# A transformer layer in split fp32r: negations later, low parts by accumulating DMA, a projection kept in HBM

## The chip, the cores and the metric

One core of a Trainium2 chip runs the whole program. The metric is the device time of one execution in microseconds. The kernel before takes 702.74 us (median of three runs, 701.41 to 702.83). TensorE (PE) multiplies, VectorE (DVE) and ScalarE (ACT) work element by element, GpSimd (POOL) has a few small operations and one DMA queue, and SyncE (SP) has the other DMA queue.

## The reference, cut to what matters

One layer on 512 tokens of width 1024, in float32, with 21 inputs:

```python
h = rms_norm(x, g_mix); z = h @ w_in      # w_in: 1024 x 3136, split into eight parts
a = mla(...)        # 4 heads: low-rank q and kv, QK-norm, rotary, dense softmax
r = hgrn2(...)      # 4 heads: gated linear recurrence in both directions, chunks of 64
x = x + concat(a, r) @ w_o
h = rms_norm(x, g_ffn)
x = x + (silu(h @ w_gate) * (h @ w_up)) @ w_down      # width 2816 inside
gate = sigmoid(rms_norm(x, g_ple) @ w_ple_gate)
x = x + gate * (p @ w_ple_proj)           # p: 512 x 256, the embeddings of the layer
```

## The kernel before, in words

Everything is held transposed: features on the 128 partitions, the 512 tokens along the free dimension. Each float32 matrix is split into a high part, rounded to the fast type fp32r, and a low part, the rest. `mm3` (L141) makes one product of three matmuls: high by high, high by low, low by high (L142, L143, L144).

A weight's parts come about in one of two ways. `split` (L132) copies the loaded tile to the high part on ScalarE (L135) and subtracts on VectorE (L136). The other way needs no VectorE: a negated copy of the high part goes into the low part's tile (ScalarE), and a DMA on GpSimd's queue loads the weight once more and adds it to that tile.

The mixer (attention, recurrence, and the products with w_in and w_o) takes its weights in 30 chunks of 1024 columns by `weights` (L148) from rings of four tiles each (WB), two chunks by `split`, 28 by DMA. `wnext` (L602) keeps three chunks ahead (AHEAD) and hands out the oldest: the call for chunk n asks for chunk n + 2. In before this includes the high part's DMA (L155), the negation (L156) and the accumulating DMA (L157), one after the other. `w_in_tile` (L608) uses a chunk in 24 matmuls, `w_in_tokens` (L621) two chunks at a time for the recurrence's values, `w_o_half` (L880) the output projection. Chunks 1 to 6 and 7 to 12 are gates and queries for two heads each, 13 to 16 values, 17 to 20 output gates, 21 to 24 and 27 to 30 w_o, 25 and 26 the projection of the embeddings. This dense stream and the latency-bound stream of attention (L373) and recurrence are generators that `merge` (L93) interleaves by their progress.

After the mixer, the feed-forward runs over 22 tiles of 128 inner features in six parts of 4, 4, 4, 4, 3 and 3. The four of part 0 (`pair_plain`, L1036) load w_gate and w_up in halves of 512 columns (`halves`, L1019) and multiply plainly; `block_sums` (L1074) forms on the side the sums of the activations that the other 18 tiles (`pair_seven`, L1096) need, where seven products of half the width take the place of eight. `down_weights` (L1154) and `down` (L1176) add each part's down projection to x. The last stage multiplies by w_ple_gate (from L1232), takes the sigmoid and the product with the embeddings' projection, and stores.

All [128, 512] tiles outside the mixer's weight rings are slots from one first-in, first-out ring (`Slots`, L58): `A` with 74 slots, to which 22 more are joined when the mixer's rings are given up. A tile that is asked for takes the slot that was given back longest ago, and its writer waits for that slot's last reader. In before the eight tiles of the embeddings' projection (`pp`, written at L952, read at L1247) keep eight slots through the whole feed-forward.

The order of the instructions on each engine and queue is not that of the program text: a planner runs a simulated timeline with its own costs when the kernel is built, takes at each moment what is ready by it, earlier text first, and fixes each queue's order; on the chip each queue then runs in that order and waits on semaphores. `issue_after` and the matmuls in `marks` pin single instructions behind others.

## Time and profile before

| what | before |
|---|---|
| median of three runs | 702.74 us |
| the profiled execution | 700.41 us |
| its span, from the first to the last instruction | 698.6 us |
| PE busy | 686.4 us, 98% |
| PE weight loads busy | 604.2 us, 86% |
| DVE busy | 509.5 us, 73% |
| ACT busy | 383.2 us, 55% |
| POOL busy | 111.1 us, 16% |
| moved by DMA | 91.18 MB, 131 GB/s on average |

Busy time of matmuls counts their modelled ends, so a pause between two matmuls is longer from start to start than in the idle column. The mixer lasts to some 295 us of the span, the plain pairs to some 350, the rest of the feed-forward to some 648, the last stage to the end.

### The profile page before, as it was taken

How to read it: one execution, taken by the hardware profiler on the slowest of the kernel's cores; microseconds unless marked ns; L12 is line 12 of the kernel's file. 1: busy time of each engine (PE TensorE's matmuls, PEld its weight loads, DVE VectorE, ACT ScalarE, POOL GpSimd, SP SyncE). 2: the span in 40 equal slices, each digit the busy share in tenths (PEclk: the TensorE clock that was granted, in tenths of full speed). 3: DMA queues.
4: the chain of work that ended last, by engine and by line, in shares of the span. 5: the costliest groups of instructions: out<-in, count | busy, mean ns of one | idle time of the engine just before them, and what ended most of it. 6: DMA issues, size and time to landing. Idle time of an engine off the chain costs nothing.

```text
span 698.6 us, 11350 instructions
## 1 busy us (share of the span) xinstructions
PE 686.4 (98%) x4170; PEld 604.2 (86%) x4170; DVE 509.5 (73%) x1031; ACT 383.2 (55%) x808; POOL 111.1 (16%) x144
## 2 busy tenths in 40 slices
PE   9999999899999999999989999999999999999997
PEld 8888887699878888878788999999999999998886
DVE  6944489797987943679987977877677578768663
ACT  7857795686645645535544554445544545546421
POOL 6233421101212222010111100001100110100000
PEclk9999999999999999999999999999999999999999
DMA  7575555543657657322456456345655664563111
GB/s 241 164 171 136 124 145 97 119 86 84 157 123 208 156 138 189 90 66 61 147 129 163 115 145 178 92 115 145 166 130 130 158 138 123 123 179 112 55 60 61
DMA packets 44264, 91.18 MB, mean 131 GB/s; under 512 B 5424, under 2 KB 11568, under 8 KB 44208
## 3 DMA queue, kind: packets, MB, share of 16 engines
q0 software_dynamic: 14976, 41.43, 28.8%
q1 hardware_dynamic: 29232, 49.02, 22.3%
q8 instruction: 33, 0.54, 0.3%
q14 instruction: 23, 0.19, 0.1%
HBM read 88.33 MB, written 2.10 MB: 129 GB/s over the span
## 4 chain that ended last, share of the span: by engine, by line
PE 86%; issue 8%; DMA 2%; ACT 2%; POOL 1%; DVE 1%; SPq 0%; POOLq 0%; ACTq 0%
PE p L144 8%; PE p L143 8%; PE p L142 8%; PE dn L143 5%; PE dn L144 5%; PE dn L142 5%; PE wi L143 4%; PE wi L142 4%; PE wi L144 4%; PE pg L144 2%; PE pg L142 2%; PE pg L143 2%; PE wo L142 2%; PE wo L144 2%; PE wo L143 2%
## 5 line engine op out<-in xcount | busy, mean ns | idle before, releaser
L142 PE MATMUL p<-bh,whi 128*128 128x256 f32 x432 | 122.3, 284 | 2.4 <-ACT whi L135 2.3
L143 PE MATMUL p<-bl,whi 128*128 128x256 f32 x432 | 121.8, 283 | 0.0
L144 PE MATMUL p<-bh,wlo 128*128 128x256 f32 x432 | 121.3, 283 | 0.0
L142 PEld LDWEIGHTS p<-bh,whi 128*128 128x128 f32 x432 | 82.7, 192 | 3.3 <-ACT whi L135 3.2
L143 PEld LDWEIGHTS p<-bl,whi 128*128 128x128 f32 x432 | 82.8, 192 | 0.1
L144 PEld LDWEIGHTS p<-bh,wlo 128*128 128x128 f32 x432 | 82.5, 192 | 0.1
L143 PE MATMUL dn<-al,whi 128*128 128x512 f32 x176 | 68.7, 390 | 0.0
L144 PE MATMUL dn<-ah,wlo 128*128 128x512 f32 x176 | 68.5, 389 | 0.0
L142 PE MATMUL dn<-ah,whi 128*128 128x512 f32 x176 | 67.7, 390 | 0.0
L1170 POOL DMA_DIRECT2D wlo<-in_w_d x32 | 27.4, 877 | 202.4 <-ACT wlo L1169 160.5
L1112 DVE TENSOR_TENSOR S<-A,A 128x512 f32<-128x512 f32 x36 | 24.4, 689 | 40.0 <-DMA A<-in_w_up 19.5
L135 ACT ACTIVATE whi<-A 128x512 fp32r<-128x512 f32 x54 | 33.6, 626 | 35.0 <-DMA A<-in_w_gate 22.8
L142 PE MATMUL wi<-hh,whi 128*128 128x512 f32 x128 | 51.2, 400 | 0.0
L144 PE MATMUL wi<-hh,wlo 128*128 128x512 f32 x128 | 50.9, 397 | 0.0
L143 PE MATMUL wi<-hl,whi 128*128 128x512 f32 x128 | 50.5, 394 | 0.0
L135 ACT ACTIVATE whi<-S 128x512 fp32r<-128x512 f32 x72 | 42.6, 623 | 10.3 <-DVE S L1112 9.0
L156 ACT ACTIVATE wlo<-whi 128x1024 fp32r<-128x1024 f32 x28 | 29.7, 1060 | 33.4 <-DMA whi<-in_w_hf 12.0
L136 DVE TENSOR_TENSOR wlo<-S,whi 128x512 fp32r<-128x512 f32 x72 | 46.3, 681 | 1.0 <-ACT whi L135 1.0
L135 ACT ACTIVATE whi<-raw 128x512 fp32r<-128x512 f32 (+2 forms) x42 | 25.5, 625 | 31.6 <-DMA raw<-in_w_up 9.7
L136 DVE TENSOR_TENSOR wlo<-A,whi 128x512 fp32r<-128x512 f32 x54 | 36.8, 682 | 3.1 <-ACT whi L135 3.1
L144 PEld LDWEIGHTS dn<-ah,wlo 128*128 128x128 f32 x176 | 33.1, 188 | 6.9
L142 PEld LDWEIGHTS dn<-ah,whi 128*128 128x128 f32 x176 | 33.0, 188 | 6.4
(342 smaller groups left out, 1840.6 us busy)
## 6 DMA issues: line engine op xcount, KB each, us to landing
A<-in_w_gate SPq DMA_DIRECT2D x36, 256.0 KB, 4.4
A<-in_w_up SPq DMA_DIRECT2D x36, 256.0 KB, 3.8
wlo<-in_w_d POOLq DMA_DIRECT2D x32, 256.0 KB, 5.3
whi<-in_w_hf POOLq DMA_DIRECT2D x14, 512.0 KB, 4.6
wlo<-in_w_hf POOLq DMA_DIRECT2D x14, 512.0 KB, 5.7
raw<-in_w_d SPq DMA_DIRECT2D x24, 256.0 KB, 2.8
x<-in_xT SPq DMA_DIRECT2D x16, 256.0 KB, 4.4
raw<-in_w_pg SPq DMA_DIRECT2D x16, 256.0 KB, 3.5
```

What stands on the lines that cost most here:

```text
L135: act.activation(hi, src, AF.Copy)
L136: eng.tensor_tensor(lo, src, hi, ALU.subtract)
L142: pe.matmul(o, lhsT=l[0], rhs=r[0], start=start, stop=False)
L143: pe.matmul(o, lhsT=l[0], rhs=r[1], start=False, stop=False)
L144: pe.matmul(o, lhsT=l[1], rhs=r[0], start=False, stop=stop)
L156: act.activation(lo[:, :cols], hi[:, :cols].bitcast(F32), AF.Copy, scale=-1.0)
L1112: dve.tensor_tensor(r[n], r[a], r[b], op)
L1170: pool.dma_start(lo[:, n], src, accum_op=ALU.add)
```

## The change

Three edits. First, in the mixer the negation and the accumulating DMA of chunks 3 to 18 (STAGED) are no longer emitted with the high part's DMA but at the next call of `wnext`, and the negation waits by a semaphore for the last matmul of the product that had been emitted last (`used`). Second, the plain pairs' weights from the third tile on get their low parts by the negated copy and an accumulating DMA on GpSimd's queue. Third, the embeddings' projection is stored to eight HBM tiles on SyncE's queue, its slots are given back, and it is loaded again ahead of the last stage.

```diff
--- before.py
+++ after.py
@@ -33,6 +33,7 @@
 WARM = 10
 NBL = 5
 LO_DVE = 2
+STAGED = 18
 FIRST = 4
 LSTEPS = "p0 p1 s0 s1 v0 p2 s2 v1 p3 s3 v2 e0 v3 e1 a0 b0 a1 c0 b1 f0 c1 f1 e2 a2 b2 e3 a3 c2 b3 f2 c3 f3"
 LORD = [(x[0], int(x[1])) for x in LSTEPS.split()]
@@ -122,6 +123,7 @@
     cpool = ctx.enter_context(tc.tile_pool(name="cpool", bufs=1))
     small = ctx.enter_context(tc.tile_pool(name="small", bufs=4))
     spool = ctx.enter_context(tc.tile_pool(name="spool", bufs=1))
+    dpool = ctx.enter_context(tc.tile_pool(name="dpool", bufs=1, space=bass.MemoryType.DRAM))
     ppool = ctx.enter_context(tc.tile_pool(name="ppool", bufs=1, space=bass.MemoryType.PSUM))
     mixer = ExitStack()
     wpool = mixer.enter_context(tc.tile_pool(name="wpool", bufs=WB))
@@ -141,9 +143,12 @@
     def mm3(o, l, r, start, stop):
         pe.matmul(o, lhsT=l[0], rhs=r[0], start=start, stop=False)
         pe.matmul(o, lhsT=l[0], rhs=r[1], start=False, stop=False)
-        pe.matmul(o, lhsT=l[1], rhs=r[0], start=False, stop=stop)
+        return pe.matmul(o, lhsT=l[1], rhs=r[0], start=False, stop=stop)
 
     nw = [0]
+    lows = deque()
+    used = []
+    later_use = mybir.DependencyInfo(mybir.DependencyClass.Sync, mybir.DependencyReason.DATA)
 
     def weights(src, cols, by_dma=False):
 
@@ -153,8 +158,18 @@
         lo = wpool.tile([P, 1024], F32R, tag="wlo", name=f"wlo{nw[0]}")
         if by_dma:
             pool.dma_start(hi[:, :cols], src)
-            act.activation(lo[:, :cols], hi[:, :cols].bitcast(F32), AF.Copy, scale=-1.0)
-            pool.dma_start(lo[:, :cols], src, accum_op=ALU.add)
+
+            def low():
+                e = act.activation(lo[:, :cols], hi[:, :cols].bitcast(F32), AF.Copy, scale=-1.0)
+                if used:
+                    tc.add_manual_dep(e.ins, used[-1].ins.name, later_use, reason="not ahead of the transfer of hi")
+                pool.dma_start(lo[:, :cols], src, accum_op=ALU.add)
+
+
+            if nw[0] <= STAGED:
+                lows.append(low)
+            else:
+                low()
         else:
             raw = wpool.tile([P, 1024], F32, tag="raw", bufs=RAWB, name=f"raw{nw[0]}")
             sp.dma_start(raw[:, :cols], src)
@@ -600,6 +615,9 @@
     nd = [0]
 
     def wnext():
+
+        while lows:
+            lows.popleft()()
         while wlist and len(ahead) < AHEAD:
             nd[0] += 1
             ahead.append(weights(*wlist.popleft(), by_dma=nd[0] > LO_DVE))
@@ -610,9 +628,10 @@
         w = wnext()
         o = BD.get("wi")
         for k in range(KT):
-            mm3(o, cut(w, k * P, k * P + P), hT[k], k == 0, k == KT - 1)
+            e = mm3(o, cut(w, k * P, k * P + P), hT[k], k == 0, k == KT - 1)
             if k % 2:
                 yield 1.3
+        used.append(e)
         z = A.get("z")
         dve.tensor_tensor(z, o, bc1, ALU.mult)
         BD.put(o)
@@ -629,9 +648,10 @@
                         a = (k % 4) * 256
                         for i in range(2):
                             j = 2 * jp + i
-                            mm3(o[i][:, :256], cut(hT[k], j * P, j * P + P), cut(ws[c], a, a + 256), k == 0, k == KT - 1)
+                            e = mm3(o[i][:, :256], cut(hT[k], j * P, j * P + P), cut(ws[c], a, a + 256), k == 0, k == KT - 1)
                         if k % 2:
                             yield 1.3
+                used.append(e)
                 for i in range(2):
                     evacuate(2 * jp + i, slice(half * 256, half * 256 + 256), o[i][:, :256])
                 BD.put(*o)
@@ -891,7 +911,8 @@
                     continue
                 for k in range(4):
                     a = ((m % 2) * 4 + k) * P
-                    mm3(o, cut(w, a, a + P), src[k], k == 0, k == 3)
+                    e = mm3(o, cut(w, a, a + P), src[k], k == 0, k == 3)
+                used.append(e)
                 dve.tensor_tensor(xT[m], xT[m], o, ALU.add)
                 banks.put(o)
                 yield 2.6
@@ -947,11 +968,15 @@
                 o = BD.get("pp")
                 for k in range(2):
                     a = (i * 2 + k) * P
-                    mm3(o, cut(w, a, a + P), pT[k], k == 0, k == 1)
+                    e = mm3(o, cut(w, a, a + P), pT[k], k == 0, k == 1)
+                used.append(e)
                 t = A.get("ppo")
                 act.copy(t, o)
                 BD.put(o)
-                pp.append(t)
+                kept = dpool.tile([P, S], F32, tag=f"pp{len(pp)}", name=f"pp{len(pp)}")
+                sp.dma_start(kept, t)
+                A.put(t)
+                pp.append(kept)
                 yield 1.3
         for hl in pT:
             A.put(*hl)
@@ -1016,13 +1041,18 @@
 
     A.join(Slots(ctx.enter_context(tc.tile_pool(name="fpool", bufs=1)), SLOTS2, "f"), 12)
 
-    def halves(src):
+    def halves(src, by_dma=False):
 
         ws = []
         for i in range(2):
             raw, hi, lo = A.get("raw"), A.get("whi", F32R), A.get("wlo", F32R)
             sp.dma_start(raw, src[:, i * 512 : i * 512 + 512])
-            split(hi, lo, raw)
+            if by_dma:
+                act.activation(hi, raw, AF.Copy)
+                act.activation(lo, raw, AF.Copy, scale=-1.0)
+                pool.dma_start(lo, src[:, i * 512 : i * 512 + 512], accum_op=ALU.add)
+            else:
+                split(hi, lo, raw)
             A.put(raw)
             ws.append((hi, lo))
         return ws
@@ -1038,7 +1068,7 @@
         nonlocal bc2, tiles_done
         zz = []
         for name in ("w_gate", "w_up"):
-            w = halves(io[name][f])
+            w = halves(io[name][f], tiles_done > 1)
             o = B.get("ff")
             with ExitStack() as behind:
 
@@ -1229,6 +1259,10 @@
         next_down()
 
 
+    for m in range(KT):
+        t = A.get("ppi")
+        sp.dma_start(t, pp[m])
+        pp[m] = t
     rs3, bc3 = token_rstd(sq3)
     for m in range(KT):
         w = halves(io["w_pg"][m])
```

## Rows read from the trace of the kernel before

**Rows 1.** The page's first part: busy us, share of span, instructions of each engine.

```profile
PE 686.4 (98%) x4170; PEld 604.2 (86%) x4170; DVE 509.5 (73%) x1031; ACT 383.2 (55%) x808; POOL 111.1 (16%) x144
```

**Rows 2.** The view by stretches: length, busy us (instructions), granted clock, DMA share, GB/s.

```profile
120.00:132.00 12.00, 9.47 (x48) 6.55 (x47) 9.17 (x29) 5.56 (x14) 2.54 (x4) 1.00 0.51 109
132.00:295.00 163.00, 163.00 (x1069) 139.27 (x1069) 116.97 (x263) 96.20 (x204) 27.88 (x37) 1.00 0.56 135
295.00:338.00 43.00, 42.38 (x188) 33.92 (x187) 37.91 (x75) 22.20 (x40) 3.38 (x4) 1.00 0.29 77
338.00:357.00 19.00, 16.23 (x91) 12.97 (x90) 17.21 (x30) 9.87 (x18) 3.38 (x5) 1.00 0.64 173
357.00:640.00 283.00, 282.84 (x1934) 263.75 (x1933) 213.25 (x371) 142.20 (x276) 32.48 (x39) 1.00 0.54 136
640.00:695.00 55.00, 53.82 (x264) 45.45 (x262) 35.27 (x64) 19.44 (x33) 1.04 (x1) 1.00 0.20 70
```

**Rows 3.** Waits of TensorE: engine, line, releaser: us in total, times, longest us.

```profile
PE pT L571 <- ACT p L557: 2.5, 2, 2.4
PE p L142 <- ACT whi L135: 2.3, 2, 1.2
```

**Rows 4.** Timeline of ScalarE, 124 to 130: start, us, line, operation, idle before it.

```profile
127.62 1.06 ACT L156 ACTIVATE wlo<-whi 128x1024 fp32r<-128x1024 f32 x1 [2.44 <-issue]
```

**Rows 5.** Line 155, 110 to 135: the high parts' transfers from issue to landing.

```profile
DMA to landing us min/median/max: 3.9/4.0/7.3
```

**Rows 6.** Timeline of TensorE, chunks six to nine.

```profile
86.40 0.39 PE L144 MATMUL wi<-hh,wlo 128*128 128x512 f32 x1
...
93.04 0.40 PE L144 MATMUL wi<-hh,wlo 128*128 128x512 f32 x1
...
93.76 0.47 PE L144 MATMUL wi<-hh,wlo 128*128 128x512 f32 x1
...
100.32 0.39 PE L144 MATMUL wi<-hh,wlo 128*128 128x512 f32 x1
```

**Rows 7.** Lines 156 and 157: the negations' duration, the low parts' transfers.

```profile
L156 ACT ACTIVATE wlo<-whi x28: 1044/1060/1074, 37.2 to 277.9; 128x1024 fp32r<-128x1024 f32 x28
...
DMA to landing us min/median/max: 5.1/5.6/8.8
```

**Rows 8.** Timeline of TensorE, 348 to 356.

```profile
348.65 0.28 PE L143 MATMUL p<-b11l,whi 128*128 128x256 f32 x1
350.04 0.39 PE L142 MATMUL p<-bh,whi 128*128 128x256 f32 x1 [1.11 <-ACT whi L135]
...
353.94 0.28 PE L144 MATMUL p<-bh,wlo 128*128 128x256 f32 x1
355.45 0.39 PE L142 MATMUL p<-bh,whi 128*128 128x256 f32 x1 [1.24 <-ACT whi L135]
```

**Rows 9.** Timeline of ScalarE, 351 to 356.

```profile
354.77 0.63 ACT L135 ACTIVATE whi<-A 128x512 fp32r<-128x512 f32 x1 [3.22 <-DMA A<-in_w_gate]
```

**Rows 10.** Waits of SyncE's DMA queue, 250 to 360.

```profile
SPq L1102 <- DVE bl L136: 6.9, 3, 4.2
```

**Rows 11.** Timeline of ScalarE, 93 to 101.

```profile
94.25 1.28 ACT L666 ACT_TABLE_LOAD   x1
...
98.80 1.28 ACT L229 ACT_TABLE_LOAD   x1
```

**Rows 12.** Groups of instructions by line, 300 to 350: busy us, mean ns, idle before.

```profile
L136 DVE TENSOR_TENSOR wlo<-raw,whi 128x512 fp32r<-128x512 f32 x11 | 7.3, 682 | 2.6 <-PE bc L195 2.6
...
L135 ACT ACTIVATE whi<-raw 128x512 fp32r<-128x512 f32 x8 | 4.9, 621 | 7.8 <-DMA raw<-in_w_up 7.8
```

**Rows 13.** The page's sixth part: DMA issues, KB each, median us to landing.

```profile
wlo<-in_w_d POOLq DMA_DIRECT2D x32, 256.0 KB, 5.3
...
raw<-in_w_pg SPq DMA_DIRECT2D x16, 256.0 KB, 3.5
```

**Rows 14.** Timeline of GpSimd, 340 to 352.

```profile
342.02 1.22 POOL L1160 DMA_DIRECT2D whi<-in_w_d  x2 [22.25 <-PE ff L143]
```

## The prediction

> **What bounds the kernel now.** I read the engine totals first, then the stretches, then what TensorE waits for, then the timelines around the few waits that are left. The reader is to see in [rows 1] that TensorE is busy for 686.4 us of a span of 698.6: no other engine comes near, and its weight loads stand at 86%. So work taken off another engine is worth only what it removes of TensorE's idle time. The change removes no product. [Rows 2] give the stretches: TensorE is full from 132 to 295 us and, but for 0.16 us, from 357 to 640, at a granted clock of 1.00, so the seven-product pairs and the down projections, which fill the long stretch, have nothing to give. It is short in three places: 12.00 - 9.47 = 2.5 us in 120 to 132, 43.00 - 42.38 = 0.6 us in 295 to 338, and 19.00 - 16.23 = 2.8 us in 338 to 357. What is left is the beginning and the end. [Rows 3] name the releasers: 2.5 us on ScalarE's softmax exponentials (L557), nearly all in one wait, and waits on ScalarE's conversions (L135).
>
> The first: ScalarE stands still for 2.44 us before the negation at 127.62 [rows 4], which is queued ahead of an exponential that TensorE's transposes need. The negation waits for the high part's transfer, and of the three such transfers in that stretch the longest took 7.3 us against a median of 4.0 [rows 5]. The second: two of TensorE's pauses show in the matmul starts of [rows 8]. From 348.65 to 350.04 and from 353.94 to 355.45 there are 1.39 and 1.51 us where two 256-column products of one stretch otherwise stand 0.12 apart; that is 1.27 + 1.39 = 2.7 us. Behind the later one ScalarE waited 3.22 us for a weight transfer [rows 9], and those transfers were issued late because SyncE's queue waited for tile slots: 6.9 us for slots that the block sums give back [rows 10]. In the same stretch VectorE is busy for 17.21 of 19 us, after 37.91 of 43 [rows 2].
>
> **The change part by part.** The sum is made against the profiled execution's 700.41 us (span 698.6 and 1.8 around it), which lies 2.33 us under the 702.74 median; I carry the difference to the median.
>
> *Negations later.* For chunks 3 to 18 the negation and the accumulating transfer are emitted at the next call of wnext and wait for the last product emitted by then. Nothing is added in number: one negation of 1.06 us on ScalarE, two transfers on GpSimd's queue for each chunk, as before. What goes is the queueing of a negation ahead of its own data: the high part was asked for a whole chunk earlier. I take the 2.5 us of [rows 3] as gained. Its bounds are nothing (VectorE or the next exponential is late instead; VectorE has 12.00 - 9.17 = 2.8 us idle there) and 2.5.
>
> What it adds is a shorter lead of the low part. The eighth chunk's negation now waits for the sixth chunk's end and the ninth's for the seventh's. I count chunks by their 24 products on TensorE. The sixth ends its last product's start at 86.40 plus a pitch of 0.23, and the eighth needs its low part at 93.76: 7.1 us. The seventh ends at 93.04 + 0.23, and the ninth needs its low part at 100.32: 7.05 us [rows 6]. The chain that has to fit is 1.06 us of negation and 5.6 us from issue to landing at the median, 8.8 at most [rows 7]: 6.7 to 9.9 us, with nothing yet for ScalarE's queue. So by the median it fits with 0.4 us to spare, and by the longest it is 2.8 us late. Other chunks stand some 9 us apart or more with attention's products between them, and have cover. ScalarE's queue is the other term: from 94.25 to 100.08 it has a table load, six sigmoids and a second load in one group [rows 11]. What waits behind the negation on ScalarE are exponentials and conversions of attention, which TensorE reads; what waits behind the accumulating transfer on GpSimd's queue are the next high part and the small powers of the norms. I take 1.2 us of new waiting, nearer the row of the median than that of the maximum: some 0.5 at the eighth and 0.7 at the ninth. The ends are -0.5 (fewer of ScalarE's waits elsewhere in the mixer, which TensorE hardly felt) and 7.4: the ninth behind the sigmoid group, 100.08 + 1.06 + 5.6 = 106.7 against 100.32, which is 6.4 us, and 1.0 at the eighth.
>
> The Trainium skill, "DMA: Bandwidth & Descriptors", section "Anatomy of one DMA — SWDGE (gpsimd) path", puts such a transfer at some 2.0 us and the bytes at 436 GB/s, by which 512 KB would be an estimated 3.2 us. The trace does not agree: its median is 5.6 us. By the page the chain would be 4.3 us, no low part would be late, and the sum would be 1.2 us better; I go by the row.
>
> *Plain pairs' low parts by transfer.* From the third tile on, six tiles of two halves: 12 subtractions of 0.68 us leave VectorE, 8.2 us; 12 copies of 0.62 us go to ScalarE, 7.5 us; 12 accumulating transfers of 256 KB go to GpSimd's queue [rows 12]. ScalarE has 43.00 - 22.20 = 20.8 us idle in 295 to 338 [rows 2], which hides its share; without that cover it would cost up to 7.5 us. A half now takes one copy and 5.3 us of landing [rows 13] where a subtraction took 0.68: 0.6 + 5.3 - 0.7 = 5.2 us more lead is wanted. GpSimd's queue is the risk: it stood for 22.25 us before the issue at 342.02, waiting for a slot [rows 14], and whatever is put behind such a wait waits too. The price is between nothing and 5.2 us at the last tile, which alone was loaded late.
>
> *The projection in HBM.* Eight stores and eight loads of 256 KB on SyncE's queue; 16 issues, and 4.2 MB in all. Eight more slots turn over during the feed-forward. A plain pair takes some 16 slots for weights and results, so eight slots are about half a pair ahead, and a pair of two tiles of 24 products at 0.23 us is 11 us: loads can go out some 5 us earlier. The late loads of the first seven-product pair were late by less (3.22 us at the worst row), and DMA is busy for only 0.29 of the stretch 295 to 338 [rows 2], so there is room for them. This pays for the longer lead of the low parts and takes most of the pauses. I take 3.0 us for both edits together: the 2.8 idle in 338 to 357 [rows 2], and a little because the busy column counts the modelled ends of products, which hides part of each pause (the 1.39 us too many between starts at 353.94 stand as 1.24 idle in [rows 8]). VectorE's relief is counted in it. The ends: nothing, if the freed slots turn up elsewhere in the ring, and 3.4, with the 0.6 of 295 to 338. The reloads stand before the last stage's weights, in a stretch where DMA is at 0.20 [rows 2]; a load of that size lands in 3.5 us [rows 13], so they cost nothing; eight in a row ahead of the weights would be some 12 us at 170 GB/s, and most of those weights are asked for more than that ahead.
>
> Sum: -2.5 + 1.2 - 3.0 = -4.3: 696.1 us for a profiled execution, 698.4 for the median.
>
> **Rivals.**
> *Both pauses go and no low part is late.* -2.5 - 3.4 = -5.9, 696.8 us. For it: the median landing fits. Against it: 0.4 us is no margin, since landings reach 8.8.
> *Only the mixer's pause goes.* The order of all queues is planned anew with a model of the times, and the eight slots may come to other tiles than those that wait; the last plain tile's low part takes the place of the late load. -2.5 + 1.2 = -1.3: 701.4 us, which can't be told from no change. For it: the bound of 5.2 us at the last tile.
> *Slower: the low part is the new wait of the mixer.* TensorE's order is fixed when the program is built; where a low part lands later than planned, everything behind it stands. Place: the eighth and ninth chunks. Price: 1.0 and 6.4 us, as above, against the 5.5 us gained: +1.9, 704.6 us. It decides from 5.5 us of such waits on, that is from the point at which ScalarE takes the ninth negation behind its sigmoid group. For it: the group lies just there, and ScalarE already waited for high parts longer than planned, so the plan's transfers are too short. Against it: the plan places the negation by its own clock, and a place ahead of the group is open at 93.3.
>
> **How the numbers follow.** Forecast 0.49, both gone 0.15, only one 0.14, slower 0.22. A measurement of this kernel tells 0.2%, 1.4 us, from no change. The first two are faster: 0.64; the third is the same: 0.14; the last slower: 0.22. The range goes from 695.0 (1.8 us under the second case, for pauses that the busy column hides) to 705.0 (just above the fourth) and leaves out the mishaps that add up. The likeliest case alone spans 696.5 to 700.5.
>
> **What would show it.** Right: no ScalarE wait on a high part's transfer near 127 us; TensorE idle under 1 us in the stretch that answers to 338 to 357; the loads of the first seven-product pair issued earlier; VectorE some 8 us less busy before it. Wrong: TensorE waiting for a transfer of a low part, which the trace before never shows; ScalarE waiting for a product before a negation while exponentials stand behind it; new pauses in the full stretch 357 to 640 or before the last stage's products.

## The result, and the profile after

The changed kernel takes 729.65 us (median; 726.25 to 733.05) where 698.4 was predicted: slower by a ratio of 1.0393 [1.0359, 1.0426], far outside the range of 695.0 to 705.0. The profiled execution is the slowest of its four runs: 733.05 us, with a span of 731.3.

The page's first part answers to [rows 1]:

```profile
PE 697.5 (95%) x4170; PEld 612.4 (84%) x4170; DVE 503.2 (69%) x1019; ACT 387.9 (53%) x820; POOL 120.0 (16%) x156
```

The products are the same 4170. TensorE is busy 697.5 - 686.4 = 11.1 us longer for them and idle (731.3 - 697.5) - (698.6 - 686.4) = 21.6 us longer. So the 32.7 us have two parts: new pauses, and the same products taking longer, which goes with a granted clock under 1.00. The view by stretches (length, busy us and instructions of PE, PEld, DVE, ACT, POOL, granted clock, DMA share, GB/s) shows both. The bounds are moved to where the same work lies, so that the six rows answer to [rows 2]:

```profile
120.00:132.00 12.00, 12.00 (x58) 9.91 (x57) 11.04 (x35) 7.92 (x22) 1.42 (x2) 1.00 0.70 135
132.00:310.00 178.00, 169.36 (x1084) 143.78 (x1083) 116.78 (x262) 101.04 (x210) 31.60 (x41) 0.98 0.62 144
310.00:355.00 45.00, 40.75 (x170) 32.27 (x169) 31.23 (x63) 27.16 (x50) 10.84 (x13) 0.92 0.60 135
355.00:375.00 20.00, 20.00 (x122) 17.90 (x121) 20.00 (x38) 12.01 (x22) 3.34 (x5) 1.00 0.50 117
375.00:672.00 297.00, 285.94 (x1917) 264.77 (x1916) 212.06 (x366) 137.73 (x273) 34.04 (x41) 0.98 0.54 139
672.00:728.00 56.00, 54.49 (x267) 45.99 (x265) 35.87 (x66) 19.71 (x34) 1.04 (x1) 1.00 0.20 69
```

The two places that the prediction wanted repaired are repaired: 120 to 132 is full, and so is 355 to 375. But the stretch that answers to 132 to 295 has 8.6 us idle where it had none, the plain pairs 4.3 where they had 0.6, and the seven-product pairs, which "have nothing to give", lose 11.1 us and clock besides. TensorE's waits (line, releaser: us in total, times, longest) answer to [rows 3]; the exponentials are gone from the list:

```profile
PE dn L144 <- ACT ah L137: 6.2, 1, 6.2
PE rT L884 <- ACT r L878: 4.9, 2, 4.5
PE ff L146 <- DMA wlo<-in_w_gate: 3.9, 1, 3.9
PE p L146 <- DVE wlo L138: 3.4, 3, 2.0
PE wt L145 <- DMA wlo<-in_w_i: 2.8, 1, 2.8
PE wi L146 <- DMA wlo<-in_w_hf: 1.9, 2, 1.7
```

Three of the six are transfers of low parts, which the trace before never showed. At [rows 4]'s place ScalarE's negation is now done early, and the next exponential waits for VectorE only:

```profile
123.82 1.06 ACT L163 ACTIVATE wlo<-whi 128x1024 fp32r<-128x1024 f32 x1
126.79 0.69 ACT L572 ACTIVATE p<-s,mx 128x512 f32<-128x512 f32 x1 [1.90 <-DVE mx L570]
```

What the others wait for stands in the timelines (start, us, engine, line, operation, idle before it and its releaser) of ScalarE, in two stretches that I put one under the other:

```profile
280.42 0.63 ACT L1051 ACTIVATE whi<-raw 128x512 fp32r<-128x512 f32 x1 [8.33 <-DMA raw<-in_w_up]
...
281.43 0.37 ACT L878 ACTIVATE r<-po,ro 128x128 f32<-128x128 f32 x1
...
657.01 1.57 ACT L137 ACTIVATE whi<-raw 128x512 fp32r<-128x512 f32 x3 [2.82 <-DMA raw<-in_w_pg]
660.23 2.08 ACT L137 ACTIVATE whi<-raw 128x512 fp32r<-128x512 f32 x4 [1.65 <-DMA raw<-in_w_pg]
662.22 0.40 ACT L1174 ACTIVATE u<-u 128x256 f32<-128x256 f32 x1
662.53 1.65 ACT L137 ACTIVATE whi<-raw 128x512 fp32r<-128x512 f32 x3
664.41 0.63 ACT L137 ACTIVATE ah<-e 128x512 fp32r<-128x512 f32 x1 [0.23 <-DVE e L1175]
```

At 280.42 ScalarE has stood for 8.33 us at a conversion whose load landed late, and the r that TensorE's transposes need is queued behind it. At the end it waits for last-stage weights while the last pair's u and ah, which TensorE's down products need, stand behind them. SyncE says why the load that the conversion at 280.42 waits for was late:

```profile
270.29 0.85 SPq L977 DMA_DIRECT2D pp<-ppo  x2
277.82 0.33 SPq L1049 DMA_DIRECT2D raw<-in_w_up  x1
```

The load goes out at 277.82, behind two stores of the projection: it got the slot that a store was still emptying, and SyncE's waits give 6.6 us for that store alone.

The table has three lengths of one profiled execution of every kernel: to the start of the mixer's last product of w_in, from there to the feed-forward's first product, and from there to the last stage's first product (starts on TensorE's timeline, subtracted). One execution differs from the next even where the instructions and their order are the same. In the first column the kernels with the mixer of before lie between 221.2 and 223.7, and "after" and "negations alone", whose engines take the mixer's instructions in the same order, are 3.7 us apart. The other two columns agree better where every engine's order is that of before (73.5 and 73.8, 353.2 and 352.3 for the kernel before and for one chunk with the order kept). So a difference of 2 to 4 us between two lengths may be chance, and the ratios, from 4 to 12 runs each, decide.

| run | mixer | to feed-forward | feed-forward | ratio [95%] |
|---|---|---|---|---|
| before | 221.7 | 73.5 | 353.2 | 1 |
| after | 229.3 | 80.9 | 370.8 | 1.0393 [1.0359, 1.0426] |
| negations alone | 225.6 | 73.9 | 352.4 | 1.0060 [1.0031, 1.0090] |
| pairs' low parts alone | 223.2 | 76.2 | 351.7 | 0.9999 [0.9980, 1.0017] |
| negations and low parts | 226.2 | 77.3 | 350.0 | 1.0046 [1.0022, 1.0069] |
| HBM alone | 223.2 | 79.6 | 374.9 | 1.0420 [1.0363, 1.0476] |
| HBM, slots held | 223.7 | 79.7 | 351.9 | 1.0068 [1.0044, 1.0093] |
| slots only, no stores | 222.7 | 77.9 | 372.4 | 1.0330 [1.0284, 1.0376] |
| HBM, late reload | 223.1 | 81.0 | 374.8 | 1.0405 [1.0375, 1.0436] |
| before, ring rotated | 223.2 | 75.4 | 351.1 | 1.0016 [0.9993, 1.0039] |
| HBM, 4 slots | 223.1 | 80.1 | 359.3 | 1.0172 [1.0128, 1.0217] |
| HBM, 8 slots in plain pairs only | 221.2 | 79.8 | 350.2 | 1.0026 [1.0008, 1.0043] |
| HBM, 8 slots in sevens only | 223.1 | 80.4 | 363.7 | 1.0237 [1.0197, 1.0276] |
| before, shorter ring | 221.5 | 73.6 | 353.2 | 0.9991 [0.9969, 1.0012] |
| HBM, block loads in order | 222.3 | 79.8 | 354.2 | 1.0094 [1.0064, 1.0125] |
| HBM, last conversions behind | 222.7 | 78.9 | 379.2 | 1.0399 [1.0359, 1.0439] |
| HBM, both pins | 223.4 | 79.8 | 354.6 | 1.0099 [1.0065, 1.0133] |
| negation of one chunk | 219.2 | 76.7 | 356.7 | 1.0023 [1.0002, 1.0043] |
| the same, order kept | 227.0 | 73.8 | 352.3 | 1.0056 [1.0038, 1.0075] |
| HBM, slots held, order kept | 222.4 | 79.9 | 352.3 | 1.0084 [1.0054, 1.0113] |

### The profile page after: what moved, and what is told of

It is laid out like the page before. It is cut to its first block, busy times and chain, and to the rows that moved or that the text cites. A ratio compares the mean times of both kernels' runs of the same rounds, so it can differ in the third digit from the quotient of the medians.

```text
span 731.3 us, 11431 instructions
## 1 busy us (share of the span) xinstructions
PE 697.5 (95%) x4170; PEld 612.4 (84%) x4170; DVE 503.2 (69%) x1019; ACT 387.9 (53%) x820; POOL 120.0 (16%) x156
## 4 chain that ended last, share of the span: by engine, by line
PE 56%; issue 16%; DMA 14%; DVE 7%; POOL 3%; ACT 3%; SPq 1%; POOLq 0%; DVEq 0%; ACTq 0%
PE p L146 6%; PE p L144 6%; PE p L145 6%; PE dn L144 4%; PE dn L145 4%; PE dn L146 4%; DMA A<-in_w_up 3%; DVE wlo L138 3%; DMA raw<-in_w_d 2%; PE wi L144 2%; PE wi L146 2%; PE pg L145 2%; PE pg L146 2%; PE pg L144 2%; PE wi L145 2%
## 5 line engine op out<-in xcount | busy, mean ns | idle before, releaser
L144 PE MATMUL dn<-ah,whi 128*128 128x512 f32 x176 | 69.4, 398 | 6.2 <-ACT ah L137 6.2
L137 ACT ACTIVATE whi<-S 128x512 fp32r<-128x512 f32 x72 | 44.0, 626 | 28.5 <-DVE S L1142 24.9
L1198 ACT ACTIVATE whi<-raw 128x512 fp32r<-128x512 f32 (+1 forms) x32 | 19.1, 598 | 37.9 <-DMA raw<-in_w_d 37.6
L145 PEld LDWEIGHTS dn<-al,whi 128*128 128x128 f32 x176 | 33.8, 192 | 6.3
```

The lines of the kernel that those rows point to most:

```text
L137: act.activation(hi, src, AF.Copy)
L144: pe.matmul(o, lhsT=l[0], rhs=r[0], start=start, stop=False)
L145: pe.matmul(o, lhsT=l[0], rhs=r[1], start=False, stop=False)
L1198: act.activation(hi[:, n], raw[:, n], AF.Copy)
```

## Experiments: one part alone

Each kernel undoes the other parts, as here (cut) for the negations and the HBM edit; the reloads go with the stores:

```diff
-            if nw[0] <= STAGED:
+            if False:
...
-                kept = dpool.tile([P, S], F32, tag=f"pp{len(pp)}", name=f"pp{len(pp)}")
-                sp.dma_start(kept, t)
-                A.put(t)
-                pp.append(kept)
+                pp.append(t)
```

Negations alone: 

> Only the mixer's edit (negation and accumulating transfer one chunk's use later); plain pairs and the projection as before. Theory A (each edit makes its own waits, and they add up): TensorE waits for low parts at the ninth and the sixteenth chunk, as in the changed kernel (5.3 us near 103 and 4.7 us near 176), the 2.5 us pause near 127 is gone, the stretch after 200 us is as before: 706 to 710 us. Rival B (no edit alone does harm; the three together crowd SyncE's and ScalarE's queues): 699 to 702 us. Rival C (any new plan of the queues costs this kernel several us wherever it falls): new waits of several us in stretches that the edit doesn't touch, after 300 us.

Pairs' low parts alone: 

> Only the plain pairs' low parts by accumulating transfer; mixer and projection as before. Theory A: the power of the feed-forward's norm stands behind an accumulating transfer on GpSimd's queue and TensorE waits some 4 us for a low part near 300 to 325, against 2 to 4 us saved in 338 to 357: 700 to 705 us. Rival B: 698 to 701 us, the pauses of 338 to 357 gone and nothing new. Rival C: new waits after 360 us.

HBM alone: 

> Only the projection kept in HBM during the feed-forward; mixer and plain pairs as before. Theory A: this is the largest part. Weight loads of the first pairs take slots that the stores give back and wait for the stores to land (TensorE idle some 4 us near 270), and in 520 to 665 us ScalarE and VectorE stand before weight conversions that are queued ahead of the elementwise work TensorE needs (10 to 16 us): 715 to 722 us. Rival B (only together): 700 to 705 us. Rival D (it is the traffic of 4.2 MB, not the queues): products wait for transfers that take longer to land than before, all medians of landing up by over 1 us.

Negations and low parts: 

> The mixer's and the plain pairs' edits, the projection in its slots as before. Theory A: the sum of both edits' own differences, 706 to 714 us, and nothing new after 360 us. Rival B: the changed kernel's waits need the projection's transfers, so 698 to 703 us.

Measured: 705.32, 701.0, 730.18 and, for the two parts without HBM, 704.47 us, ratio 1.0046 [1.0022, 1.0069]. The HBM edit carries the loss; the negations lose 0.6% and the low parts do nothing that can be told. The HBM edit lost 8 us more than I had expected at most (722), and the first two parts together 1.5 us less than at least (706). By itself the HBM edit is as slow as the whole change (729.65), so the parts do not simply add up. Negations alone, ninth chunk (ScalarE, GpSimd and TensorE):

```profile
97.77 1.28 ACT L244 ACT_TABLE_LOAD   x1
99.06 1.07 ACT L163 ACTIVATE wlo<-whi 128x1024 fp32r<-128x1024 f32 x1
100.16 1.84 ACT L140 ACTIVATE qkh<-qkT,vec 128x512 fp32r<-128x512 f32 x3
...
100.43 0.87 POOL L166 DMA_DIRECT2D wlo<-in_w_hf  x1 [6.57 <-ACT wlo L163]
...
101.78 0.47 PE L144 MATMUL s<-qkh,qkh 128*128 128x512 f32 x1 [0.58 <-DVE qkl L141]
102.81 0.50 PE L145 MATMUL s<-qkl,qkh 128*128 128x512 f32 x1 [0.56 <-DVE qkl L141]
105.69 0.51 PE L146 MATMUL wi<-hh,wlo 128*128 128x512 f32 x1 [1.43 <-DMA wlo<-in_w_hf]
...
175.27 0.39 PE L145 MATMUL wt<-wlo,hh 128*128 128x256 f32 x1 [2.04 <-DMA wlo<-in_w_i]
```

This is the slower rival, at its place: the negation comes right behind the sigmoid group and its table load, the low part goes out at 100.43, TensorE waits for it at 105.69, and the scores behind the negation are late too. The sixteenth chunk, which the prediction didn't name, loses 2.04 us to a late low part too. There is no sigmoid group: its negation, at 168.06, stands behind exponentials for which ScalarE had waited 4.69 us on VectorE. After that pause the granted clock is 0.91 in 160 to 180.

## Experiments: transfers or slots

```diff
 held: stores and reloads as they are, no slot given back until the reloads
-                A.put(t)
+                held.append(t)
...
+    A.put(*held)
     for m in range(KT):
         t = A.get("ppi")
 slots only: given back, no store; the end loads tiles of w_pp in the projection's place
-                sp.dma_start(kept, t)
-        sp.dma_start(t, pp[m])
+        sp.dma_start(t, io["w_pp"][m % 2][:, m // 2 % 2 * 512 : m // 2 % 2 * 512 + 512])
 late reload: each reload behind halves(io["w_pg"][m])
 rotated: the kernel before, with A.free.rotate(-8) behind the projection
```

Held: 

> The projection is stored to HBM and loaded again as in the change (mixer and plain pairs as before), but its eight slots are held until the reload, so the slot ring of the feed-forward is that of before. Theory R (the cost comes from the eight slots: with them the planner puts weight conversions earlier into ScalarE's and VectorE's queues, ahead of the elementwise work that TensorE needs, and the loads land later than planned): 701 to 706 us, no TensorE waits of over 1 us in 360 to 640. Rival T (the stores and reloads themselves, by traffic and by their places in SyncE's queue): 720 to 732 us.

Slots only: 

> The eight slots are given back at once, but nothing is stored; at the end eight tiles of a weight are loaded in place of the projection, so the output is not the reference's. Theory R: 720 to 730 us, with waits at the last pair's elementwise work and in the seven-product pairs. Rival T: the stores' half of the cost goes, 702 to 715 us; in any case the wait of a weight load for a store's landing near 270 to 285 us is gone.

Late reload: 

> As the projection's edit alone, but each reload stands behind the last stage's weights of its tile instead of all eight ahead of them. Theory R: 726 to 732 us, the wait of some 6 us near 656 stays, since it comes from conversions queued ahead. Rival T: the reloads held up the last stage's weights, so the waits after 640 us go: 718 to 723 us.

Rotated: 

> The kernel before with the ring of free slots turned by eight places behind the projection; nothing else, no slot more. Theory R: the phase of the ring doesn't matter, 700 to 704 us. Rival P (any shift of which slot waits for which reader costs this kernel much): over 708 us.

Measured: 706.12, 724.72, 730.17 and 702.7 us (ratios of the last two 1.0405 [1.0375, 1.0436] and 1.0016 [0.9993, 1.0039]). The transfers cost 0.7%, the eight slots by themselves 3.3%; the reloads' place and the ring's phase are not it. The table says where: held loses its 6 us before the feed-forward, slots only lose 19 us inside it. They lose 4 us before it too, with no store, so what is lost there is not a matter of stores alone; the last experiment separates the two.

## Experiments: how many slots, and where

```diff
 four: every second slot held until the reloads
 plain pairs only: eight free slots taken out ahead of the seven-product pairs
+            extra = [A.free.popleft() for _ in range(8)]
 sevens only: held through the plain pairs, put back there
+            A.put(*held)
 shorter ring: the kernel before
-SLOTS2 = 22
+SLOTS2 = 18
```

Four: 

> As the projection's edit alone, but only four of the eight slots are given back, the other four held until the reload. Theory R (more slots, more run-ahead of the plan, more harm): about half of the ring's cost, 712 to 720 us. Rival P (the harm comes from which tile's slot a load inherits, which depends on the ring's exact length, not on its being longer): anything from 703 to 735 us, not in between by need.

Plain pairs only: 

> The eight slots turn over during the plain pairs only and are taken out of the ring again ahead of the seven-product pairs. From the trace of the projection's edit alone TensorE's extra idle time is some 6 us in 260 to 340, 4 in 340 to 380, 10 in 380 to 640 and 8 after it. Theory R and rival P alike: the last two go, 706 to 712 us. If the end's waits come from the mixer's end or the plain pairs by a shift: over 715 us.

Sevens only: 

> The eight slots are held through the plain pairs and join the ring for the seven-product pairs only. Theory R and rival P alike: the store's cost of the run with held slots (706 us) and the 18 us after 380: 718 to 726 us.

Shorter ring: 

> The kernel before with four slots less in the feed-forward (18 joined instead of 22), nothing else. Theory R: fewer slots, less run-ahead: loads later, a little slower at most, 700 to 708 us, and no conversions ahead of the last elementwise work. Rival P: as bad as a longer ring, 710 to 730 us, with loads that wait for slots of late elementwise tiles.

Measured: 714.34, 703.23, 719.77 and 701.1 us, the last at 0.9991 [0.9969, 1.0012]. None, four and eight slots give 706, 714 and 730 us. The loss sits in the seven-product pairs, and the kernel before has slots to spare: it is no slower with four fewer. The two stretches do not add up, though. With the slots in the sevens only, 14 of the 24 us over the held slots show, and with the slots in the plain pairs only, which came out 3 us better than I had expected, none. So with the slots in both, the sevens lose more; I did not follow that up.

## Experiments: the order of the loads

More room should not hurt. What it changes is the order in which SyncE issues the loads, since that queue's order is planned when the kernel is built. For three pairs it stands so in the built kernels (pairs count from 0 and a to d are a pair's four blocks as written, so 8a is the first block of the ninth seven-product pair; a d by itself is a down weight):

```
before               7c 7d 7a 7b 8a 8b d d 8c 8d d 9b 9a 9c d 9d 10b d
HBM alone            7a 8c 7d 7c d 9a 8b 8d 9d 8a 10a d 9b d 9c d 10d
HBM, loads in order  7a 7b 7c 7d d 8a 8b 8c 8d 9a d 9b d 9c 9d 10a d
```

In the long ring 8a, which that pair's first product needs, stands behind 9a and 9d of the next pair. Two kernels undo what such an order does, at SyncE or at the end of ScalarE's queue, and a third does both:

```diff
 block loads in the order in which they are written
+            with ExitStack() as behind:
+                if blocks_read:
+                    behind.enter_context(tc.issue_after(blocks_read[-1].ins))
+                blocks_read.append(sp.dma_start(r[n], io[name][f][:, i * 512 : i * 512 + 512]))
 last stage's conversions behind the split of the last pair's result
+        with tc.issue_after(ends[0].ins), tc.issue_after(ends[1].ins):
+            w = halves(io["w_pg"][m])
```

Loads in order: 

> The projection in HBM alone (730.2 us), with one thing pinned: the block loads of the seven-product pairs stand on SyncE in the order in which they are written (first pair first, four blocks each). In the longer ring their order is mixed: a block of the next pair stands ahead of one that the present pair still lacks. Theory (order on the in-order queues is what the longer ring spoils, SyncE's first): TensorE's pauses of 2.2, 1.5 and 1.5 us at 483, 537 and 552 us, whose conversions wait for a block's landing, go, the granted clock is 1.00 from 440 to 640 us, 716 to 724 us; the 6 us ahead of the last pair's down product stay. Rival (the slots themselves: each load waits for a late elementwise reader of its slot, in whatever order): 727 to 733 us, pauses as they are.

Last conversions behind: 

> The projection in HBM alone (730.2 us), with one thing pinned: the conversions of the last stage's weights on ScalarE and VectorE stand behind the split of the last seven-product pair's result. Theory (what stands ahead of that pair's elementwise work in ScalarE's queue is the end's 6 us): the wait of the down product for ah of 6 us falls under 2 us and the end's granted clock rises, 722 to 725 us. Rival (the pair itself comes late, or the last stage then waits for its weights instead): 728 to 732 us.

Both: 

> Both pins, block loads in written order and the last conversions behind the last pair, on the projection in HBM alone. If the order of the queues is what the eight more slots cost: 708 to 718 us, as much as both pins alone together, and near the 706 us of the slots held back. If the slots cost through their readers: over 724 us.

Measured: 708.76, 730.12 (ratio 1.0399 [1.0359, 1.0439]) and 708.52 us (1.0099 [1.0065, 1.0133]). The plan with the block loads in order takes back 21 of the 24 us that the slots cost; it gave more than I expected, the end's pause included: TensorE's wait for ah is 1.2 us instead of 5.8. Of the stretch from 480 to 560 us the views show HBM alone, then the loads in order:

```profile
480.00:560.00 80.00, 74.65 (x493) 69.19 (x492) 55.31 (x95) 34.99 (x69) 6.91 (x8) 0.96 0.45 118
```

```profile
480.00:560.00 80.00, 80.00 (x561) 75.22 (x561) 59.92 (x102) 40.67 (x80) 10.36 (x12) 1.00 0.55 139
```

HBM alone, SyncE's longest wait around this place, its issues from 472 us, and below them what ScalarE and TensorE make of it:

```profile
SPq L1195 <- DVE u L1168: 13.0, 1, 13.0
...
472.00 0.33 SPq L1195 DMA_DIRECT2D raw<-in_w_d  x1
472.43 0.42 SPq L1132 DMA_DIRECT2D A<-in_w_gate  x1
474.38 0.33 SPq L1132 DMA_DIRECT2D A<-in_w_up  x1
475.14 0.33 SPq L1132 DMA_DIRECT2D A<-in_w_gate  x1
477.23 1.57 SPq L1132 DMA_DIRECT2D A<-in_w_gate  x2
...
482.65 0.63 ACT L137 ACTIVATE whi<-A 128x512 fp32r<-128x512 f32 x1 [3.67 <-DMA A<-in_w_gate]
...
485.86 0.58 PE L146 MATMUL p<-b11h,wlo 128*128 128x256 f32 x1 [2.02 <-DVE wlo L138]
```

These are d 9a 8b 8d 9d 8a: 8a is the second of the two loads at 477.23, and ScalarE and TensorE wait for it. The down weight at 472.00 had held the queue for 13.0 us, waiting for a slot that VectorE's u still used. With the loads in order the same pair's four blocks go out at 465.20 to 467 (the last row also holds 9a):

```profile
465.20 0.33 SPq L1136 DMA_DIRECT2D A<-in_w_gate  x1
465.58 0.99 SPq L1136 DMA_DIRECT2D A<-in_w_up  x2
466.68 0.85 SPq L1136 DMA_DIRECT2D A<-in_w_gate  x2
```

and TensorE is busy for all of 380 to 640 us. So it is shown that the plan with the loads in order is 21 us faster with the same slots. The pin moved other engines, too: up to the feed-forward every order is that of HBM alone, but in it VectorE's and ScalarE's instructions differ from HBM alone's in about one place of seven and one of nine, besides SyncE's. Three things speak for SyncE's order as the cause. The waits above lead back to block loads. In the shorter ring VectorE's and ScalarE's orders differ from those of before more than that, and nothing is lost. And in the built kernels the number of times that a pair's block is issued ahead of a block of an earlier pair goes with the times: none in the shorter ring, the plain pairs only and the loads in order (701, 703, 709 us), 2 in before and held (703, 706), 18 with four slots (714), 23 to 25 with eight in the sevens (720 to 730). A kernel that has HBM alone's order on every engine but SyncE was not run. My second theory for the end fell: with the last conversions moved back the pause stayed, and ScalarE stood 6.90 us at a down weight's load instead:

```profile
661.03 0.52 ACT L137 ACTIVATE whi<-raw 128x384 fp32r<-128x384 f32 x1 [6.90 <-DMA raw<-in_w_d]
```

So ScalarE's order only chose which late load is waited for; the lateness came from SyncE, where this load went out at 654.98, behind six loads for the last stage. Why the planner mixes the order with more slots I argue only: by its own clock the other pair's slot is free first, and with few slots there is no other pair's load to choose.

## Experiments: one chunk's negation, and orders kept

```diff
 one chunk: only the fourteenth, whose negation stood in front of the exponentials
-            if nw[0] <= STAGED:
+            if nw[0] == 14:
...
 order kept: every engine's instructions chained in the order of the kernel before
+        for a, b in zip(names, names[1:]):
+            tc.add_manual_dep(traced[b], a, mybir.DependencyInfo(mybir.DependencyClass.NoSync, mybir.DependencyReason.DATA), reason="as before")
```

One chunk: 

> The kernel before with the mixer's edit for the fourteenth chunk alone, whose negation stood for 2.44 us in front of the exponentials at 127 us; every other chunk's negation is where it was, the ninth's too. Theory (the mixer's edit loses because the ninth and sixteenth chunks' negations come behind the sigmoid group, and gains 2.4 us at the fourteenth): 699 to 701 us, ratio 0.995 to 0.998, TensorE's wait for p at 126.7 us under 0.6 us and no new pause over 0.5 us up to 150 us. Rival (the later low part is waited for there as well): 702 to 704 us.

One chunk, order kept: 

> The mixer's edit for the fourteenth chunk alone, as in the run before it (703.1 us, where the mixer ended 2.5 us earlier and all of it was lost again from 220 to 350 us), but now every engine's instructions stand in the order of the kernel before, pinned one behind the other; only that chunk's negation, nine places later on ScalarE, and its low part's transfer on GpSimd are moved. Theory (a local edit is lost because the planner deals the orders of the later stages anew): the 2.4 us stay, 697.5 to 699.5 us, ratio 0.994 to 0.998. Rival (the later stages give an earlier start back whatever their order, since they wait for something else): 700 to 702 us; or the later low part is itself the price: 702 to 704 us.

HBM with slots held, order kept: 

> The projection stored in HBM and read back with its eight slots held until then (706.1 us, of which 6 us were lost between 222 and 303 us, where the stores go), but now every engine's instructions up to the last stage's stand in the order of the kernel before, pinned; the eight stores are put between SyncE's loads where the planner likes. Theory (the 0.7% is the changed order too): 700 to 703 us, ratio under 1.004, feed-forward's first product at 295 to 297 us. Rival (the stores themselves, in SyncE's queue ahead of the first pairs' loads): 704 to 708 us, first product at 301 us or later.

Measured: 703.12, 705.48 and 707.56 us. One chunk ends the mixer 2.5 us earlier, as expected (2.0 us earlier than the earliest of the other kernels with the mixer of before), and 225.6 - 219.2 = 6.4 us earlier than all sixteen in the run with the negations alone: that is the price of the other fifteen, as far as two executions tell it. But it gives 3.2 + 3.5 us back behind the mixer, where its edit touches nothing. The trace places all of it before the end of the feed-forward's first 96 products (into ff), which take 29.0 instead of 24.9 us, with TensorE waiting 1.7 us for hl and 1.2 for sq; from there to the last stage it is 299.8 us, in before 300.3. With the order kept the two lengths are as before (73.8 and 352.3), but the mixer loses, for the negation now waits with work behind it:

```profile
140.19 2.01 ACT L164 ACTIVATE wlo<-whi 128x1024 fp32r<-128x1024 f32 x2 [6.16 <-PE wi L146]
...
144.93 0.68 ACT L140 ACTIVATE qkh<-qkT,vec 128x512 fp32r<-128x512 f32 x1
...
145.66 0.50 PE L144 MATMUL s<-qkh,qkh 128*128 128x512 f32 x1 [4.08 <-ACT qkh L140]
```

So I expected wrongly twice. In this order, too, the later negation was put where work follows that TensorE needs, so the run doesn't show what the 2.5 us are worth with the later stages as they were. A later negation needs a place in ScalarE's order where nothing urgent follows; and which part of the new order makes the start of the feed-forward slower is not settled.

Held with the order kept still loses 6.4 us before the feed-forward, so here my rival was right: it is the stores themselves, and not a changed order. DMA issues from 240 to 300 us (KB each, median us from issue to landing), of the kernel before and then of this one:

```profile
whi<-in_w_or POOLq DMA_DIRECT2D x4, 512.0 KB, 5.3
...
raw<-in_w_up SPq DMA_DIRECT2D x4, 256.0 KB, 3.9
```

```profile
whi<-in_w_or POOLq DMA_DIRECT2D x4, 512.0 KB, 6.4
...
pp<-ppo SPq DMA_DIRECT2D x8, 256.0 KB, 5.5
...
raw<-in_w_up SPq DMA_DIRECT2D x3, 256.0 KB, 7.6
```

Weights on GpSimd's queue land a microsecond later at the median while SyncE's stores run. The one that counts, issued at 262.11, took 8.9 us where its counterpart of before took 5.7 (8.2 in HBM alone, whose median of 5.2 doesn't show it). ScalarE waits for it with the projection's copies behind it, and TensorE for one of these copies:

```profile
271.05 1.06 ACT L163 ACTIVATE wlo<-whi 128x1024 fp32r<-128x1024 f32 x1 [5.67 <-DMA whi<-in_w_or]
...
PE pp L144 <- ACT ppo L974: 3.0, 1, 3.0
...
283.43 1.16 ACT L137 ACTIVATE whi<-raw 128x512 fp32r<-128x512 f32 x2 [4.38 <-DMA raw<-in_w_up]
```

The Trainium skill, "DMA: Bandwidth & Descriptors", section "Queues, rings and completion order", says that each DMA engine takes turns between the queues that have work for it. The later landing, 6.4 against 5.3 us, agrees with that; no run here shows the turns themselves. After the 3.0 us the granted clock is 0.83 in 260 to 280, where before has 1.00. That the stores cost some 6 us is shown; that they cost it by way of these landings I argue from the timelines. No version beat the kernel before; the nearest are the low parts alone, the shorter ring and the rotated ring, which can't be told from it.

## Why the prediction was wrong

**The step that failed** is "The projection in HBM". It read eight more slots as loads "some 5 us earlier", took 3.0 us of gain from them together with the low parts, and said of the reloads that they cost nothing; of the stores it priced only their bytes. Measured by itself this edit costs 4.2%, about 29 us: some 24 from the slots, of which a plan with the block loads in order takes back 21, and 5 to 6 from the stores. The reloads did cost nothing that can be told (730.17 against 730.18 us with each behind its weights). The loads did go out earlier, but not evenly: in HBM alone the first two blocks of the first seven-product pair are asked for 8 us after the feed-forward's first product (41 and 46 in before), the next two at 33 and 34 (47 and 48), and from the fifth on 2 to 5 us earlier or not at all. Some of the gain was there, too: with the slots in the plain pairs only the feed-forward takes 350.2 us, against 351.1 to 353.2 in the executions with its ring and its code as before or the slots held. The row that I used for it, SyncE's 6.9 us of waiting for slots [rows 10], did show a lack of slots, but at one place. That the later stretch was full [rows 2] should have been read as something to lose: any edit that has the queues planned anew risks it. The sentence that would show this stood under "Wrong" (new pauses in 357 to 640), with no term and no price; and the rival that named the new plan of all queues ("Only the mixer's pause goes") priced it as a gain that stays away, not as a loss.

**Negations later.** The 2.5 us at 127 came off, as predicted. The lost lead was put at 1.2 us; it is some 6.4 in the run with the negations alone, and more in the whole change's execution, which ends the mixer 3.7 us later. The ninth chunk stands behind the sigmoid group, as the bound of 7.4 in the same paragraph has it, and the rival built on it had this place, the mechanism and the sign. That its price for the ninth chunk, 6.4, is also the sum measured is luck: there TensorE loses 1.43 us for the low part and 0.58 and 0.56 for the scores, the sixteenth chunk, which the rival doesn't have, loses 2.04, and the granted clock of 0.91 in 160 to 180 accounts for most of the rest. I gave the rival 0.22 because a place ahead of the group was open at 93.3; the plan did not take it. The landing was about right (5.6 us at the median in [rows 7]; the ninth's took from 100.43 to 105.69): what ate the lead was ScalarE's queue.

**Plain pairs' low parts.** Alone they take 1.5 us off the feed-forward and lose 2.7 ahead of it by the table, but the execution profiled (703.14 us) is 2.1 above their median; the ratio of 0.9999 says that they are worth nothing in sum. In the whole change a price shows: TensorE waits 3.9 us for a low part of w_gate. That is inside the 0 to 5.2 that were given, but not at the last tile: it is the first tile that gets its low part by transfer, at 327.79, and this transfer took 7.5 us from issue to landing where the sum had 5.3.

**The forecast's shape.** Every price was a wait at a place that the edits touch. Most of the 29 us, the 21 of the block loads, came from a place that they don't touch.

## What to carry to other kernels

Where queues' orders are planned when the kernel is built, a longer ring of tile slots is a change to every queue: compare the built orders of the two kernels before pricing anything, and pin loads that one consumer needs together in the order of their use. A stage that TensorE fills is not safe, it is what the plan can spoil. An instruction that is made to wait costs what stands behind it in its queue, so its new place has to be named together with the wait.

## What the runs showed of the hardware

The pauses cost more than their length. Before, the granted clock is 1.00 in all six stretches of [rows 2]. After, two of the stretches of 20 us with a pause of 4 to 6 us in or into them show:

```profile
320.00:340.00 20.00, 16.12 (x66) 12.95 (x65) 6.26 (x16) 6.55 (x11) 4.54 (x5) 0.83 0.62 131
...
660.00:680.00 20.00, 14.90 (x55) 12.09 (x56) 17.16 (x29) 11.74 (x21) 0.00 (x0) 0.83 0.57 202
```

TensorE ran part of them at the lower of its two levels (1.2 instead of 2.4 GHz), where 512-column products start 0.42 us apart instead of 0.23 (from 666.12 to 666.54 us behind the second pause, and from 658.10 to 658.32 ahead of it). Over the run TensorE is busy for 11.1 us longer with the same products, beside 21.6 us of new idle time: half as much again. Not every pause brings this: with the negations alone, 100 to 120 us has 2.6 us of idle time and a granted clock of 1.00. A forecast of a pause of several microseconds should carry it.
